# Hybrid conformer/SSD layer on one core: four projection tiles open while h comes in, and x's mean square found token by token

## The chip, the core and the metric

The kernel runs on one core of one Trainium2 chip. The metric is the device time of one execution in microseconds (us); three runs of the kernel before gave 1263.3 to 1267.06 us, with a median of 1263.39 us. The engines are named as in the profile: PE is TensorE, PEld its weight loads, DVE is VectorE, ACT is ScalarE, POOL is GpSimd, and SP is the engine whose queue issues all DMAs here.

## The reference, cut to what matters

One layer of a diffusion backbone with a Conformer branch and a Mamba-2 (SSD) branch, 512 latent tokens x, 256 context tokens ctx, 1024 channels. The change touches the beginning only:

```python
h  = modulate(rmsnorm(x,   norm1_w), mod[0],   mod[1])      # mod   = adaln(c, w_ada, b_ada)
hc = modulate(rmsnorm(ctx, norm1_w), mod_c[0], mod_c[1])    # mod_c = adaln(c_ctx, ...)
proj = h @ w_in                                             # x/B/C, dt, z, GLU and gate columns
xs, B, C, dt_f, dt_b = ssd_inputs(proj)                     # conv of width 5 + SiLU; softplus(dt)
# chunked scan of 8 groups in both directions, starting from the final state of the scan over ctx
```

`rmsnorm(x)` is x / sqrt(mean(x*x over the channels) + 1e-6), times a weight. After the scan come the gated merge, an output projection and a squared-ReLU MLP.

## The kernel before, in words

Channels lie on the partitions and tokens along the free dimension, so a projection tile is 128 output channels by 512 tokens. Each product is made in three passes over exact high and low parts (`gemm`, lines 114 to 116): for each of eight slices k of the input channels, high weights times high activations, high times low, low times high. So a tile of x takes 24 matmuls of 128x512, and a tile of ctx 24 of 128x256. A weight tile comes as `raw` by DMA (line 96, two buffers), ACT casts it to the high part `whi` (line 105), and DVE subtracts to get `wlo` (line 106). `whi` and `wlo` have two buffers each, so a third weight tile can be split only when the products of the first are over.

The order of instructions on each engine is set by a scheduler that works on priorities: normally the order in which the code is written, moved by `later(n)` (what is inside gives way to the next n instructions, and comes earlier for a negative n). Each engine then runs its list strictly as listed.

The beginning: x is loaded (`x_sb`), its squares are added up over the channel tiles into `acc_rx` (line 208), and `rsqrt_mean` turns the sum into 1/sqrt: one matmul with ones sums over the partitions and gives the sum to all 128 of them (`sum`, line 147), and then every step runs on 128x512 elements (`rv` line 133, a square root on ACT, the reciprocal `r` line 136, `rq` lines 138 and 139, `rx` line 142). For ctx the kernel uses `rsqrt_rows` instead: matmuls of 128x1 sum the squares token by token (`rows`, line 157), so that the steps `rt` (lines 161 to 166) run on 128x2 elements, a diagonal matrix `dg` is built (line 168), and a matmul with ones spreads it over the partitions (`spread`, line 171).

The modulation vectors of x and ctx come in four steps, i = 0 to 3. Each step loads a 2 MB block of the adaLN weights (`ablk`, four DMAs, two buffers), makes 32 small matmuls (`aps`, line 252, eight for each DMA, here called a quarter), copies and transposes the result (`arow` on ACT, `apt` on PE), and finishes two channel slices of `mod` on DVE; then `enter` makes the two slices of h (`xr`, `hh` on ACT, `hl` on DVE). Beside the steps three projection tiles are open: dt with step 0, B of group 0 with step 1, C with step 2. Each open tile multiplies the slices of h as they appear. The high and low weights of dt and of B lie in a tile of their own, `wd`, those of C in `whi` and `wlo`. When h is whole, the two x tiles of group 0 (`Xt`, called X0 and X1 below) are made in one go each.

Then every x tile of B, C and X goes through `taps5` on DVE (lines 370 and 374: a convolution of width 5 read from PSUM), hc is made from ctx and `rc`, the ctx tiles follow, and `dt_part` runs a long chain: softplus as a polynomial, running sums `cf` by two scans (lines 327 and 328), their exponential `ecf`, the decays `dec`. `cf` and `ecf` go to DRAM (`s_cf`, lines 343 and 344, four writes for each), the decays too (`s_dec`, lines 346 and 348), and come back spread over the partitions as `decb` (line 349) and, for each head and direction, as `cfb` (line 507, three buffers). In `ssd`, group by group, PE transposes (`bps`, `xps`) and makes states (`sps`) in a PSUM pool of three tiles, ACT copies out (`Bk`, `xt`, `hst`), DVE makes the states that enter the chunks (`hst`, lines 497 and 498, with `decb`), ACT makes the exponents `e` from `cfb` (line 510), POOL and DVE make `Cd` from `cfb` (line 523), and PE makes the outputs `yps` (line 536 from `Cd` and `hst`, line 532 from `e` and `xt`).

The lines that the change touches lie in `rsqrt_rows`, `stat`, the loop of the four steps, and `xbc_first`.

Of the kernel before, what the change touches and what calls it, by code (L numbers as in the profile page):

```python
# [8 lines left out]
F32 = mybir.dt.float32  # L9
# [5 lines left out]
P = 128  # L15
D = 1024
KT = 8
T = 512
TC = 256
# [3 lines left out]
EPS = 1e-6  # L23
# [3 lines left out]
# columns of the packed per-channel vectors  # L27
# [8 lines left out]
# order of the input projection's 128-column tiles  # L36
# [6 lines left out]
# the groups beside which the first tiles of the convolution module run  # L43
GLU_AT = (0, 1, 2, 3, 4)
# the steps of the first modulation vectors beside which the first three weight tiles come, and ctx
BEGIN_AT, CTX_AT = (0, 1, 2), 3
# products that keep the tensor engine's clock up before there is work
WARM = 22
# the products of C and the decays (direction, head of the pair) that VectorE does, the rest are GpSimd's
DECAYS_V = ((0, 1),)  # L50
# how far instructions move in the order of priority
# [5 lines left out]
def build(tc, xT, ctxT, cond, crow, wada1, wada2, vecs, hv, cst, w_in, w_co, w_so, w_o, w_1, w_2, outT):  # L57
    nc = tc.nc
    with ExitStack() as es:
# [26 lines left out]
        @contextmanager  # L86
        def later(n):
            """what is traced inside gives way to the next n instructions"""
            tc.cur_priority += n
            yield  # L90
            tc.cur_priority -= n

# [37 lines left out]
        def rsqrt_mean(ps, n, cnt, r=None):  # L130
            """1/sqrt(sum/cnt + EPS) of a sum broadcast over the partitions"""
# [18 lines left out]
        def rsqrt_rows(parts, n, cnt, pool, out=None):  # L150
            """the same of the sum of several tiles, found token by token and then spread over the partitions"""
            nch = n // P
            s = pool.tile([P, T], F32, name="rows", tag="pm")
            for i, part in enumerate(parts):
                with later(ROWS_LATER):
# [36 lines left out]
        with tc.tile_pool(name="st", bufs=1) as st:  # L192
# [10 lines left out]
            def stat(src, n, acc, out):  # L203
# [5 lines left out]
                if n == TC:  # L209
                    return rsqrt_rows([acc], n, D, pm, out)  # L210
                return rsqrt_mean(allsum(acc, n, pm), n, D, out)
# [12 lines left out]
            # products of nothing: the tensor engine's clock halves when it idles  # L224
# [10 lines left out]

            for i in range(4):
# [3 lines left out]
                if i == BEGIN_AT[0]:  # L240
                    begin(W_DT, py.tile([P, T], F32, name="ps", tag="py"), wd[:, 0], wd[:, 1])
                if i == BEGIN_AT[1]:
                    begin(W_GRP, ps_big(), wd[:, 2], wd[:, 3])
                if i == BEGIN_AT[2]:
                    begin(W_GRP + 1, ps_big())
                if i == CTX_AT:
                    for j, c in enumerate(ctx):
                        nc.sync.dma_start(c, ctxT[:, 2 * j:2 * j + 2])
# [26 lines left out]
        wx = [load_w(w_in[W_GRP + 2 + j], early=0) for j in range(2)]  # L275
# [18 lines left out]
        def dt_part(ps, pc):  # L294
            conv = bigt("conv")
            # rows: heads forward, the same again, heads backward, the same again; the first of each hold
            # chunks 0 to 2, the second chunk 3 and the context
# [10 lines left out]
            # softplus: max(v, 0) + log1p(u), u = exp(-|v|), log1p(u) = 2 atanh(u / (2 + u))  # L308
# [13 lines left out]
            # running sums within the chunks and within the context, backward ones from the end  # L322
# [22 lines left out]
            # step s: chunk s forward, chunk 3 - s backward  # L345
# [41 lines left out]
        def xbc_first():  # L387
            """the first group's, all of x's part before ctx's"""
            Bt, Ct, X0, X1 = (xbc_tile(tag, n) for tag, n in (
                ("Bt", T + TC), ("Ct", T), ("Xt", T + TC), ("Xt", T + TC)))  # L390
            (w_dt, ps_dt, _), (w_b, ps_b, _), (_, ps_c, _) = begun
# [3 lines left out]
            for j, o in enumerate((X0, X1)):  # L395
                ps = ps_big()
                gemm(ps, wx[j], rh)
# [39 lines left out]
        def ssd(g, Bt, Ct, X, Z):  # L437
            ch = lambda t, c: t[:, c * P:(c + 1) * P]
            # B^T C of every chunk, for both directions
# [9 lines left out]
            # B by token  # L449
# [6 lines left out]
            # x by token, and times what reaches the chunk's end  # L456
# [420 lines left out]
```

## Time and profile before

| what | us |
|---|---|
| median of 3 runs (lowest, highest) | 1263.39 (1263.3, 1267.06) |
| span of the profiled execution | 1264.2 |
| PE busy in it | 1220.7 |
| DVE busy | 953.7 |
| ACT busy | 667.4 |
| first product of an open tile starts | 23.43 |
| first product of the SSD outputs (`yps`) starts | 113.69 |

The profiled execution has no time of its own in the list of runs; its span, from the first to the last instruction, stands in its place. PE busy is the union of spans with modelled ends, so that a matmul of 128x512 shows about 0.4 us though the next starts 0.23 us after it. An idle time in a timeline stands in square brackets behind the instruction that ended it, with what released that instruction.

### The profile page before, as it was taken

To read this page: it belongs to the slowest core of one execution; us is meant where nothing else is said; L and a number is where in the kernel's file an instruction comes from. 1 tells how busy PE (TensorE), PEld (TensorE's weight loads), DVE (VectorE), ACT (ScalarE), POOL (GpSimd) and SP (SyncE) were. 2 spreads that over 40 slices of the span, in tenths; PEclk is the share of its full clock that TensorE was granted. 3 is DMA by queue.
4 is the path that set the end of the run, shared out by engine and by line. 5 is a ranking of instruction groups with operands and counts; after the bars stand their busy time and mean duration, and the time that the engine had idled before them with its cause. 6 is when DMAs were issued, how large, how long until landed. Compare 5 with 4: busy or idle time off the path is not lost.

```text
span 1264.2 us, 17493 instructions
## 1 busy us (share of the span) xinstructions
PE 1220.7 (97%) x6665; PEld 995.6 (79%) x6665; DVE 953.7 (75%) x1567; ACT 667.4 (53%) x1124; POOL 108.9 (9%) x74
## 2 busy tenths in 40 slices
PE   6998999999999899999999999999999999999997
PEld 3786778777787778787888877778998888888886
DVE  6797689999999999998999798885843343443444
ACT  4557888686776748868453452134431331331442
POOL 0001222121020302124000000000000000000000
PEclk8999999999999999999999999999999999999999
DMA  9424363343342424333363357964222333233332
GB/s 363 142 67 133 137 198 128 120 146 106 121 159 93 158 83 147 112 134 117 109 193 126 119 188 258 305 196 153 62 65 86 100 100 92 92 100 101 96 104 67
DMA packets 56260, 169.96 MB, mean 134 GB/s; under 512 B 6640, under 2 KB 9584, under 8 KB 56048
## 3 DMA queue, kind: packets, MB, share of 16 engines
q1 hardware_dynamic: 56176, 168.85, 41.0%
q8 instruction: 52, 0.85, 0.3%
q14 instruction: 32, 0.26, 0.1%
HBM read 162.27 MB, written 6.55 MB: 134 GB/s over the span
## 4 chain that ended last, share of the span: by engine, by line
PE 65%; DVE 20%; DMA 8%; issue 3%; ACT 3%; SPq 0%; POOL 0%; DVEq 0%; ACTq 0%; POOLq 0%
PE ps L114 20%; PE ps L115 19%; PE ps L116 19%; DVE conv L575 5%; DVE wlo L106 3%; DVE Xt L374 3%; DMA aw<-in_wada_dram 2%; DMA cfb<-s_cf 2%; PE yps L536 2%; PE yps L532 2%; PE sps L485 1%; DMA yr<-s_y 1%; DVE aw L675 1%; DMA raw<-in_w_dram 1%; ACT whi L105 1%
## 5 line engine op out<-in xcount | busy, mean ns | idle before, releaser
L105 ACT CAST whi<-raw 128x1024 fp32r<-128x1024 f32 x163 | 170.9, 1049 | 320.6 <-PE ps L115 291.5
L106 DVE TENSOR_TENSOR wlo<-raw,whi 128x1024 fp32r<-128x1024 f32 x163 | 203.8, 1251 | 84.3 <-ACT whi L105 76.1
L114 PE MATMUL ps<-hh,whi 128*128 128x512 f32 x632 | 258.0, 408 | 2.3 <-DVE Xt L374 2.1
L116 PE MATMUL ps<-hh,wlo 128*128 128x512 f32 x632 | 255.4, 404 | 2.3 <-DVE wlo L106 2.2
L115 PE MATMUL ps<-hl,whi 128*128 128x512 f32 x632 | 256.7, 406 | 0.0
L575 DVE SCALAR_TENSOR_TENSOR conv<-sg,V,conv 128x480 f32<-128x480 f32 (+14 forms) x240 | 173.3, 740 | 2.6 <-ACT conv L569 1.1
L114 PEld LDWEIGHTS ps<-hh,whi 128*128 128x128 f32 x632 | 119.4, 189 | 30.8 <-issue 7.2
L116 PEld LDWEIGHTS ps<-hh,wlo 128*128 128x128 f32 x632 | 119.4, 189 | 30.7 <-DVE wlo L106 4.7
L115 PEld LDWEIGHTS ps<-hl,whi 128*128 128x128 f32 x632 | 119.6, 189 | 26.5 <-issue 3.7
L711 DVE SCALAR_TENSOR_TENSOR x<-ps,mod,x 128x512 f32<-128x512 f32 (+1 forms) x48 | 31.7, 660 | 100.1 <-PE ps L116 100.1
L510 ACT ACTIVATE e<-cfb,cfT 128x128 f32<-128x128 f32 x256 | 83.9, 391 | 36.8 <-PE yps L532 17.5
L523 POOL TENSOR_TENSOR Cd<-Ct,cfb 128x512 f32<-128x512 f32 x48 | 72.6, 1518 | 313.0 <-DMA cfb<-s_cf 250.3
L116 PE MATMUL ps<-h2h,wlo 128*128 128x512 f32 (+1 forms) x240 | 89.8, 375 | 0.0
L115 PE MATMUL ps<-h2l,whi 128*128 128x512 f32 (+1 forms) x240 | 89.8, 375 | 0.0
L114 PE MATMUL ps<-h2h,whi 128*128 128x512 f32 (+1 forms) x240 | 89.4, 375 | 0.0
L115 PE MATMUL ps<-gl,whi 128*128 128x512 f32 x224 | 88.4, 395 | 0.0
L114 PE MATMUL ps<-gh,whi 128*128 128x512 f32 x224 | 88.2, 394 | 0.0
L116 PE MATMUL ps<-gh,wlo 128*128 128x512 f32 x224 | 87.9, 392 | 0.0
L374 DVE SCALAR_TENSOR_TENSOR Xt<-ps,V,Xt 128x255 f32<-128x255 f32 (+3 forms) x128 | 74.2, 605 | 3.9 <-ACT Xt L370 3.6
L114 PE MATMUL ps<-hc,whi 128*128 128x256 f32 x184 | 52.5, 285 | 3.1 <-DVE Xt L374 3.1
L115 PE MATMUL ps<-hc,whi 128*128 128x256 f32 x184 | 52.4, 285 | 0.0
L116 PE MATMUL ps<-hc,wlo 128*128 128x256 f32 x184 | 52.1, 283 | 0.0
(259 smaller groups left out, 2417.5 us busy)
## 6 DMA issues: line engine op xcount, KB each, us to landing
raw<-in_w_in_dram SPq DMA_DIRECT2D x81, 512.0 KB, 3.6
cfb<-s_cf SPq DMA_DIRECT2D x64, 512.0 KB, 4.4
raw<-in_w_dram SPq DMA_DIRECT2D x64, 512.0 KB, 3.5
aw<-in_wada_dram SPq DMA_DIRECT2D x64, 256.0 KB, 4.3
ablk<-in_wada_dram SPq DMA_DIRECT2D x16, 512.0 KB, 8.6
raw<-in_w_so_dram SPq DMA_DIRECT2D x16, 512.0 KB, 3.7
s_y<-yt SPq DMA_DIRECT2D x16, 256.0 KB, 2.2
yr<-s_y SPq DMA_DIRECT2D x16, 256.0 KB, 3.6
```

What stands on the lines that cost most here:

```text
L105: nc.scalar.copy(hi, raw)
L106: nc.vector.tensor_tensor(lo, raw, hi, ALU.subtract)
L114: nc.tensor.matmul(ps, lhsT=whi[:, k, :], rhs=rhi[:, k, t0:t1], start=start and k == 0, stop=False)
L115: nc.tensor.matmul(ps, lhsT=whi[:, k, :], rhs=rlo[:, k, t0:t1], start=False, stop=False)
L116: nc.tensor.matmul(ps, lhsT=wlo[:, k, :], rhs=rhi[:, k, t0:t1], start=False, stop=stop and k == KT - 1)
L374: nc.vector.scalar_tensor_tensor(o[:, lo:hi], ps[:, lo + d:hi + d], vcol(V_SCW + 5 * ch + j), o[:, lo:hi], ALU.mult, ALU.add)
L510: nc.scalar.activation(ch(e, c), cb_[:, 0, c * P:(c + 1) * P], AF.Relu, bias=cfT[:, c, hd:hd + 1], scale=-1.0)
L523: (nc.vector if (d, r) in DECAYS_V else nc.gpsimd).tensor_tensor(Cd, Ct, cb_[:, 1, :], ALU.mult)
L532: nc.tensor.matmul(o, lhsT=xt[:, c, hr, :], rhs=ch(Ms[r], c), start=False, stop=True, skip_group_check=True)
L536: nc.tensor.matmul(o, lhsT=hst[:, s, k, hr * 64:hr * 64 + 64], rhs=ch(Cs[k][r], c), start=k == 0 and c == 0, stop=False, skip_group_check= ...
L575: nc.vector.scalar_tensor_tensor(o[:, :, lo:hi], u[:, :, lo + d:hi + d], wv(j), o[:, :, lo:hi], ALU.mult, ALU.add)
L711: nc.vector.scalar_tensor_tensor(x1[:, j, a:b], ps[:, a:b], mod[:, gcol + j, 0:1], x1[:, j, a:b], ALU.mult, ALU.add)
```

## The change

It has four parts. `stat` uses `rsqrt_rows` for x too, with a delay of 0 in the order of priority instead of 60. The weights of dt are asked for ahead of the first adaLN block, those of B with step 0, those of C with step 1. A fourth tile, X0 of group 0, is open from step 2 on, in the third and last tile of the PSUM pool `pp` (B and C have the other two, dt is in another pool), so that X1 gets the tile that B's taps have left. X0 is then not made in `xbc_first` any more, and only X1's weights are loaded behind the loop. (In the changed file some lines have moved by one or two, so line 252 is 251 there, 349 is 348.)

```diff
-BEGIN_AT, CTX_AT = (0, 1, 2), 3
+BEGIN_AT, CTX_AT = (-1, 0, 1, 2), 3
...
-        def rsqrt_rows(parts, n, cnt, pool, out=None):
+        def rsqrt_rows(parts, n, cnt, pool, out=None, late=ROWS_LATER):
...
-                with later(ROWS_LATER):
+                with later(late):
...
-                if n == TC:
-                    return rsqrt_rows([acc], n, D, pm, out)
-                return rsqrt_mean(allsum(acc, n, pm), n, D, out)
+                return rsqrt_rows([acc], n, D, pm, out, ROWS_LATER if n == TC else 0)
...
+            begin(W_DT, py.tile([P, T], F32, name="ps", tag="py"), wd[:, 0], wd[:, 1])
             for i in range(4):
...
-                if i == BEGIN_AT[0]:
-                    begin(W_DT, py.tile([P, T], F32, name="ps", tag="py"), wd[:, 0], wd[:, 1])
                 if i == BEGIN_AT[1]:
                     begin(W_GRP, ps_big(), wd[:, 2], wd[:, 3])
                 if i == BEGIN_AT[2]:
                     begin(W_GRP + 1, ps_big())
+                if i == BEGIN_AT[3]:
+                    begin(W_GRP + 2, ps_big())
...
-        wx = [load_w(w_in[W_GRP + 2 + j], early=0) for j in range(2)]
+        wx = [begun[3][0], load_w(w_in[W_GRP + 3], early=0)]
...
-            (w_dt, ps_dt, _), (w_b, ps_b, _), (_, ps_c, _) = begun
+            (w_dt, ps_dt, _), (w_b, ps_b, _), (_, ps_c, _), (_, ps_x, _) = begun
...
             for j, o in enumerate((X0, X1)):
-                ps = ps_big()
-                gemm(ps, wx[j], rh)
+                ps = ps_big() if j else ps_x
+                if j:
+                    gemm(ps, wx[j], rh)
                 taps5(o[:, :T], ps, j, EVICT_FIRST)
```

The priorities of everything behind are the same numbers, but the scheduler lays out the lists anew. Three places follow.

**First place: PE up to the first product of an open tile** (`aps` is a block of adaLN products, `apt` its transpose, `ps<-hh,wd` the first product). Before:

```order
L147 MATMUL sum<-acc_rx,C 128x512
L252 MATMUL aps<-ablk,sc 32x128 x32
L258 MATMUL apt<-C,arow 128x128
L252 MATMUL aps<-ablk,sc 32x128 x24
L114 MATMUL ps<-hh,wd 128x512
```

Now:

```order
L157 MATMUL rows<-C,acc_rx 128x1 x4
L171 MATMUL spread<-dg,C 128x512
L251 MATMUL aps<-ablk,sc 32x128 x32
L257 MATMUL apt<-C,arow 128x128
L251 MATMUL aps<-ablk,sc 32x128 x16
L114 MATMUL ps<-hh,wd 128x512 x2
L115 MATMUL ps<-hl,wd 128x512
```

The one sum of x has become four products of one column and a spread; both stand ahead of the first adaLN block; two quarters of the second block instead of three stand ahead of the first product of dt.

**Second place: PE around the norm of ctx** (`rows<-C,acc_rc` sums the squares of ctx, `spread<-dg,C` spreads the result, `whi` and `wlo` are the weights of C, X0 and X1). Before, the sums, and 26 products of 128x512 counted from the second sum on before the spread:

```order
L114 MATMUL ps<-hh,whi 128x512
L115 MATMUL ps<-hl,whi 128x512
L116 MATMUL ps<-hh,wlo 128x512
L157 MATMUL rows<-C,acc_rc 128x1
L114 MATMUL ps<-hh,whi 128x512
L157 MATMUL rows<-C,acc_rc 128x1
L115 MATMUL ps<-hl,whi 128x512
L116 MATMUL ps<-hh,wlo 128x512
```

Now:

```order
L114 MATMUL ps<-hh,whi 128x512
L115 MATMUL ps<-hl,whi 128x512
L116 MATMUL ps<-hh,wlo 128x512
L157 MATMUL rows<-C,acc_rc 128x1 x2
L114 MATMUL ps<-hh,whi 128x512
L115 MATMUL ps<-hl,whi 128x512
L116 MATMUL ps<-hh,wlo 128x512
L114 MATMUL ps<-hh,whi 128x512
L171 MATMUL spread<-dg,C 128x256
L115 MATMUL ps<-hl,whi 128x512
```

The spread stood behind 26 products after the sums, and now stands behind four, which are the first of X1; on DVE the split of X1's weights stands ahead of the steps from the sums to `dg`, and five taps of B, C and X0 stand between these steps, as five did before.

**Third place: SP's queue and ACT where group 0 begins** (`s_cf`, `s_dec` are the writes of the sums and decays, `decb` and `cfb` the loads of what they wrote, `e` the exponents made from `cfb`). SP before:

```order
L346 DMA s_dec<-dec 32x3
L348 DMA s_dec<-dec 32x1 x3
L343 DMA s_cf<-conv 32x384
L344 DMA s_cf<-conv 32x128
L343 DMA s_cf<-conv 32x384
L344 DMA s_cf<-conv 32x128
L349 DMA decb<-s_dec 128x192
L96 DMA raw<-in_w_in_dram 128x1024
L507 DMA cfb<-s_cf 128x1024 x4
```

SP now:

```order
L342 DMA s_cf<-conv 32x384
L343 DMA s_cf<-conv 32x128
L342 DMA s_cf<-conv 32x384
L343 DMA s_cf<-conv 32x128
L345 DMA s_dec<-dec 32x3
L347 DMA s_dec<-dec 32x1
L507 DMA cfb<-s_cf 128x1024 x2
L347 DMA s_dec<-dec 32x1 x2
L507 DMA cfb<-s_cf 128x1024 x2
L348 DMA decb<-s_dec 128x192
L96 DMA raw<-in_w_in_dram 128x1024
```

ACT before:

```order
L455 COPY Bk<-bps 128x512
L455 COPY Bk<-bps 128x256
L384 ACT_TABLE_LOAD
L384 ACTIVATE Bt<-Bt 128x768
L477 COPY xt<-xps 128x512
L491 COPY hst<-sps 128x512
L477 COPY xt<-xps 128x512
L510 ACTIVATE e<-cfb,cfT 128x128 x5
```

ACT now:

```order
L455 COPY Bk<-bps 128x512
L455 COPY Bk<-bps 128x256
L510 ACTIVATE e<-cfb,cfT 128x128 x4
L512 ACTIVATE e<-e 128x512
L510 ACTIVATE e<-cfb,cfT 128x128 x4
L383 ACT_TABLE_LOAD
L383 ACTIVATE Bt<-Bt 128x768
L477 COPY xt<-xps 128x512 x2
L491 COPY hst<-sps 128x512
```

On SP all eight writes of `s_cf` now stand ahead of the decays, and four loads of `cfb` ahead of `decb`. On ACT eight exponents from `cfb` have moved ahead of SiLU of the next group's B, the copies of `xt` and that of the first state `hst`.

## Rows read from the trace of the kernel before

**Rows 1.** The page, part 1: busy time of each engine, share of the span, instructions.
```profile
PE 1220.7 (97%) x6665; PEld 995.6 (79%) x6665; DVE 953.7 (75%) x1567; ACT 667.4 (53%) x1124; POOL 108.9 (9%) x74
```

**Rows 2.** Windows over the program: stretch, length, busy time (instructions) by engine, TensorE clock, DMA share, GB/s.
```profile
50.00:100.00 50.00, 46.11 (x260) 39.77 (x259) 47.48 (x103) 30.10 (x47) 0.00 (x0) 1.00 0.22 66
...
100.00:150.00 50.00, 45.20 (x271) 34.87 (x270) 37.82 (x66) 38.00 (x81) 9.46 (x7) 0.97 0.47 144
...
150.00:640.00 490.00, 477.93 (x2797) 385.81 (x2796) 458.65 (x736) 357.84 (x665) 92.74 (x60) 1.00 0.40 130
```

**Rows 3.** Timeline of PE, 10 to 24 us: start, length, instruction, idle before and releaser.
```profile
12.04 1.86 PE L147 MATMUL sum<-acc_rx,C 128*128 128x512 f32 x2 [3.82 <-DVE acc_rx L208]
...
13.83 2.85 PE L252 MATMUL aps<-ablk,sc 128*32 128x128 f32 x64
...
17.07 0.33 PE L258 MATMUL apt<-C,arow 128*128 128x128 f32 x1 [0.40 <-ACT arow L256]
...
20.82 0.65 PE L252 MATMUL aps<-ablk,sc 128*32 128x128 f32 x16 [0.64 <-DMA ablk<-in_wada_dram]
...
23.43 0.80 PE L114 MATMUL ps<-hh,wd 128*128 128x512 f32 x1 [1.96 <-ACT hh L217]
```

**Rows 4.** Timeline of DVE (VectorE), 13 to 24 us.
```profile
15.33 3.35 DVE L136 RECIPROCAL r<-r 128x512 f32<-128x512 f32 x1 [0.70 <-ACT r L135]
...
18.60 1.16 DVE L106 TENSOR_TENSOR wd<-raw,wd 128x1024 fp32r<-128x1024 f32 x1
...
21.11 0.69 DVE L142 SCALAR_TENSOR_TENSOR rx<-rq,r 128x512 f32<-128x512 f32 x1
```

**Rows 5.** Windows in the beginning, columns as in rows 2.
```profile
12.00:16.00 4.00, 3.96 (x50) 2.34 (x54) 1.36 (x2) 1.93 (x3) 0.00 (x0) 0.57 1.02 417
...
18.00:22.00 4.00, 1.94 (x48) 1.16 (x48) 3.97 (x8) 0.01 (x1) 0.00 (x0) 1.00 1.04 412
...
24.00:28.00 4.00, 3.56 (x23) 2.52 (x23) 3.67 (x7) 1.30 (x3) 0.00 (x0) 0.50 1.03 410
```

**Rows 6.** Timeline of PE near the end, the last norm.
```profile
1257.43 0.67 PE L171 MATMUL spread<-dg,C 128*128 128x256 f32 x2 [1.88 <-DVE dg L168]
```

**Rows 7.** Timeline of PE, 52 to 60 us, the norm of ctx.
```profile
52.72 0.28 PE L157 MATMUL rows<-C,acc_rc 128*128 128x1 f32 x2
...
58.88 0.60 PE L171 MATMUL spread<-dg,C 128*128 128x256 f32 x2
```

**Rows 8.** Timeline of DVE, 50 to 60 us.
```profile
50.84 0.75 DVE L374 SCALAR_TENSOR_TENSOR Bt<-ps,V,Bt 128x510 f32<-128x510 f32 x1
...
53.64 0.15 DVE L161 TENSOR_SCALAR rt<-rows 128x2 f32<-128x2 f32 x1
...
57.32 0.42 DVE L168 TENSOR_TENSOR dg<-C,rt 128x256 f32<-128x256 f32 x1
```

**Rows 9.** Timeline of SP's queue, 98 to 114 us.
```profile
97.62 1.36 SPq L348 DMA_DIRECT2D s_dec<-dec  x3
...
104.58 0.34 SPq L349 DMA_DIRECT2D decb<-s_dec  x1
...
105.50 2.77 SPq L507 DMA_DIRECT2D cfb<-s_cf  x3
```

**Rows 10.** Timeline of ACT (ScalarE), 98 to 114 us.
```profile
104.30 1.28 ACT L384 ACT_TABLE_LOAD   x1 [0.85 <-DVE Bt L374]
...
107.91 0.58 ACT L491 COPY hst<-sps 128x512 f32<-128x512 f32 x1 [0.89 <-PE sps L485]
...
112.29 1.71 ACT L510 ACTIVATE e<-cfb,cfT 128x128 f32<-128x128 f32 x5 [3.31 <-DMA cfb<-s_cf]
```

**Rows 11.** Timeline of PE, 98 to 114 us, and PE's waits up to 150 us (total, times, longest).
```profile
113.69 0.43 PE L536 MATMUL yps<-Cd,hst 128*64 128x128 f32 x2 [3.15 <-POOL Cd L523]
...
PE yps L536 <- POOL Cd L523: 4.8, 2, 3.1
```

**Rows 12.** DMA issues by line, 90 to 115 us: count, size, median time to landing.
```profile
s_cf<-conv SPq DMA_DIRECT2D x4, 48.0 KB, 3.7
```

## The prediction

> **What bounds the kernel now.** I read the page's busy times first: PE is busy in 97% of the span [rows 1]. Then I read the windows, since an average says nothing of one stage. From 150 to 640 us PE is busy for 477.93 of 490 us [rows 2]: there PE is the bound, and this change alters none of its work there. From 50 to 100 us both PE (46.11 of 50) and DVE (47.48 of 50) are nearly full, and from 100 to 150 us PE stands still for 4.8 us [rows 2]. So a gain at the start is kept only if it reaches about 150 us: past that point PE has its fixed list to work through, and what is saved by then stays saved.
>
> Third, I read the timelines of the beginning. The sum of x's squares is made on PE at 12.04 [rows 3], and 1/sqrt is ready at 21.80, where `rx` ends [rows 4]. In between lie a reciprocal over 128x512 that takes 3.35 us and, in DVE's list, a weight subtraction of 1.16 us that two small steps of the norm stand behind [rows 4]. The first product of an open tile starts at 23.43 [rows 3]. It runs at 1.2 GHz: from 24 to 28 us the granted clock is 0.50, after a stretch in which PE had only quarters of adaLN products with idle times between them (1.94 us busy in 18 to 22) [rows 5].
>
> Last, I read the other end of the beginning. The first load of `cfb` is issued at 105.50, behind `decb` at 104.58, which waited for the decays issued from 97.62 on [rows 9]. It lands when ACT starts on it, at 112.29 [rows 10], and PE, which has waited 3.15 us, starts the outputs of group 0 at 113.69 [rows 11].
>
> **The change, part by part.** The sum is made against the profiled execution, whose span is 1264.2 us; that is 0.8 above the median of the three runs, 1263.39.
>
> *The norm of x.* Four sums of one column replace the sum of 1.86 us. A pair of records takes 0.28 us for one such sum at full clock [rows 7], so four take 0.6 to 1.2; PE has idled for 3.82 us before [rows 3], so I take 1.2: 13.24. Between such sums and a spread PE waited 1.88 us where nothing else was in the way [rows 6]; `dg` for 512 tokens instead of 256 adds about 0.3 (0.42 for 256 columns [rows 8], 0.69 for an operation of 512 [rows 4]). So the spread starts at 15.4 and, priced like the old sum, ends at 17.3. `rx` is there by 18, almost 4 us earlier. But that is not the gain. The first adaLN block now stands behind the spread, so it runs from 17.3 to 20.1 instead of from 13.83 (2.85 us, [rows 3]; 3.5 if PE stays slow). Copy and transpose of it ended 0.7 us behind it, at 17.40 [rows 3]: now 20.8. The path from `rx` to the first product took 1.63 us (21.80 to 23.43), one step of which is no longer in it; I take 1.3. First product at 22.1: **-1.3 us** (bounds -0.6 and -1.9).
>
> *The clock.* PE is now busy almost without a break from 15.4 to 22. I expect it to be at 2.4 GHz when the products start. That saves half of the 4 us at 0.50 [rows 5]: **-2.0** (bounds 0 and -3).
>
> *The loads.* From 12 to 28 us the queues move 410 to 417 GB/s [rows 5], so 512 KB take 1.3 us, and each later adaLN block comes that much later. This costs nothing: PE waited only 0.64 us for the last such quarter before the products [rows 3], and comes to it over 3 us later now. Without that cover it would be 1.3. The Trainium skill ("Perfetto Trace Analysis", the note on HBM above 100%) puts the ceiling of one core's 16 DMA engines at about 435 GB/s; the rows agree, and by it alone fetching ahead would only push other loads back, which would make this part +1.3 instead of 0.
>
> *Four open tiles.* The products are the same 120. By the two lists B is now finished after 84 of them instead of 67 (I counted them to the last product on `wd`). Between the sums of ctx and the spread 26 products took 6.0 us [rows 7], 0.23 each, so 17 more are 3.9 us. One more quarter lies behind the first product (0.65, [rows 3]), and the last block is cut into small pieces, for which I take 0.5 (0 to 1.4). B's taps began at 50.84 [rows 8]; they begin 3.9 + 0.65 + 0.5 - 1.3 - 2.0 = 1.8 us later, at 52.6.
>
> *A new wait.* X0's 24 products used to cover three things: B's taps leaving their PSUM tile for X1, the split of X1's weights, and the steps from the sums of ctx to `dg`, 4.1 us on DVE from 53.64 to 57.74 [rows 8]. Now only four products of X1 stand between sums and spread, so PE will wait at X1's first product and at the spread, 4 us together (bounds 0 and 4.4). Who waits behind it: the rest of X1, then `rc`, hc and every ctx product. X1's products end later, but the spread itself comes only some 0.6 us later, since DVE sets it now as it nearly did before. DVE has 2.5 us of idle in 50 to 100 us [rows 2], and everything it needs lies ready earlier than before (C and X0 end with B); I let it win back the 1.8. So dt's sums end when they did, **0** (bounds -1 and +3.7).
>
> *The queue.* `cfb` needs `s_cf` alone. The eight writes are now in front: four more issues (1.7 us) and a landing of 3.7 [rows 12] from about the time of 97.62 give 103.0, and they no longer queue behind the exponentials of the decays, some 0.5 earlier: 102.5, **-3.0** for the first `cfb` (bounds 0 and -4). It lands at 109.3 instead of 112.29.
>
> *ACT's list.* That is given back. Eight exponents (1.71 us for five [rows 10], so 2.7), one operation of 128x512 (0.6) now come ahead of what ended with the copy of `hst`. That stretch ran from 104.30 to 108.49 with 0.89 of waiting [rows 10], 3.3 net, and a second copy (0.6) joins it. The first state is copied at 109.3 + 2.7 + 0.6 + 3.3 + 0.6 = 116.5, and the next one needs two operations of 0.7 on DVE: 117.9. At that place in its list (a first bundle of outputs, nine more products done) the old kernel was at 113.69 + 0.43 + 9 x 0.46 at half clock = 118.3. So **-0.4**. PE's second wait for `Cd`, 4.8 - 3.15 = 1.65 us [rows 11], has a load behind it that is asked for earlier now: **-1.0** (0 to -1.65).
>
> Behind that the lists keep their shape group by group, and from the LayerNorm of the conv branch on they are the same: 0, with up to 2 either way, as PE has 12 us of idle from 150 to 640 [rows 2] which new lists deal out anew. The sum is -1.4 from 1264.2, and 0.8 less for the median: **1262.0 us**. I count 0.3% (3.8 us) as what a measurement of this kernel can tell from no change.
>
> **The rivals.** *All of it is kept.* If `cfb` lands at 107 or before and the wait at the spread is covered, PE loses the wait of 3.15, the half clock behind it (9 x 0.23 = 2.1) and the second wait of 1.65 [rows 11], 6.9 at most; I take -5.5: 1257.9. For it speaks the gain of 3 us in the queue; against it ACT's list.
>
> *ACT stands in front of a load (slower).* ACT is where PE's next PSUM tile and first state come from, and it now waits for `cfb` with these copies behind it. Before, it had made them by 108.49, 3.8 us ahead of the landing [rows 10]. If `cfb` lands as late as it did, 112.29, the state comes at 119.5 and outputs start at 120.9, 2.6 later than 118.3; PE meanwhile stands at its third state product and restarts at half clock, 2.1 more. That is +4.7: 1268.1. It decides from a landing of about 109.5 on. The Trainium skill ("TensorE: Matmul & The Clock Gate", Architectural detail) says that ScalarE's and VectorE's queues are strictly first in, first out; the subtraction in rows 4 agrees, and by that rule alone this rival would be the outcome whenever the load is late.
>
> *The fourth tile does nothing.* It may only trade X0's cover for an earlier X0 [rows 7, 8], and the start may be lost to DVE's full list: +-0, 1263.4.
>
> **How the numbers follow.** My forecast has 0.47, the gain kept 0.26, ACT's wait 0.19, nothing 0.08. A tail of the forecast on each side passes 0.3%: faster 0.29, same 0.49, slower 0.22. The range takes in the two outer cases: 1256.5 to 1268.
>
> **What would show it.** Right: the first product near 22.1 with a granted clock of 1.00 from 24 to 28; PE waiting some 4 us for DVE at X1 and at the spread; `cfb` issued near 102.5; `hst` copied near 116.5. Wrong: a clock of 0.50 again, no wait at the spread, `cfb` still behind 105, or a difference that arises past 150 us, where I see none.

## The result and the profile after

The changed kernel takes 1270.65 us (median of 20 runs, 1268.06 to 1277.68); the kernel before, run beside it, 1263.74 us (20 runs, 1260.08 to 1273.31). The ratio is 1.005, with a 95% interval of 1.0036 to 1.0063: the change costs 6 us, half a per cent, where 1262.0 with a range of 1256.5 to 1268 was forecast. The profiled execution has a span of 1270.3 us (1264.2 before).

The page, part 1, of the changed kernel [rows 1]: every engine does almost what it did.

```profile
PE 1225.7 (96%) x6673; PEld 999.9 (79%) x6673; DVE 953.9 (75%) x1568; ACT 659.8 (52%) x1119; POOL 110.2 (9%) x74
```

The start, as the timeline of PE shows it [rows 3]:

```profile
12.35 1.87 PE L157 MATMUL rows<-C,acc_rx 128*128 128x1 f32 x8 [4.57 <-DVE acc_rx L208]
...
16.29 2.08 PE L171 MATMUL spread<-dg,C 128*128 128x512 f32 x2 [2.08 <-DVE dg L168]
...
23.88 0.73 PE L114 MATMUL ps<-hh,wd 128*128 128x512 f32 x2 [0.29 <-ACT hh L215]
```

The windows of the start and of 50 to 100 us [rows 5, 2]:

```profile
12.00:16.00 4.00, 1.87 (x8) 1.78 (x8) 1.58 (x7) 2.79 (x5) 0.00 (x0) 0.50 1.03 420
...
24.00:28.00 4.00, 3.42 (x40) 1.97 (x40) 3.46 (x6) 0.53 (x1) 0.00 (x0) 1.00 0.97 348
50.00:100.00 50.00, 43.60 (x222) 36.76 (x221) 43.94 (x94) 29.54 (x46) 0.00 (x0) 0.93 0.13 42
```

The clock is at 2.4 GHz when the products start, as forecast, but the first of them starts at 23.88 instead of 23.43. And from 50 to 100 us, where DVE was nearly full, it now has 6.06 us of idle time instead of 2.52. So I looked for what DVE waits for. Timeline of DVE before, from the last block's `mod` to the last scan of the running sums:

```profile
44.23 0.17 DVE L260 TENSOR_TENSOR mod<-apt,V 128x8 f32<-128x8 f32 x1 [3.98 <-PE apt L258]
...
94.43 0.95 DVE L328 TENSOR_TENSOR_SCAN conv<-conv,dysq 64x384 f32<-64x384 f32 x1
```

and after:

```profile
49.96 0.17 DVE L259 TENSOR_TENSOR mod<-apt,V 128x8 f32<-128x8 f32 x1 [7.83 <-PE apt L257]
...
57.56 1.53 DVE L373 SCALAR_TENSOR_TENSOR Bt<-ps,V,Bt 128x510 f32<-128x510 f32 x2 [1.85 <-ACT Bt L369]
...
102.22 0.95 DVE L327 TENSOR_TENSOR_SCAN conv<-conv,dysq 64x384 f32<-64x384 f32 x1
```

The last `mod` is 5.7 us later, and DVE stands idle for its transpose for 7.83 us; B's taps begin 6.7 us later (50.84 before, [rows 8]); the sums end at 103.17 instead of 95.38, 7.8 us later. One window from the last `mod` to the end of the sums, first before, then after:

```profile
44.23:95.38 51.15, 48.82 (x265) 41.69 (x264) 48.15 (x100) 31.29 (x49) 0.00 (x0) 1.00 0.21 63
```

```profile
49.96:103.17 53.21, 46.81 (x236) 39.40 (x235) 47.05 (x98) 30.11 (x46) 0.00 (x0) 0.94 0.16 49
```

DVE has 47 to 48 us of work there in 51 to 53 us, so most of what is late at the last `mod` is late at the sums. (Over all runs below the stretch takes 50.3 to 55.1 us.) But DVE's wait just ahead of the taps, 1.85 us, is for B itself. B's last product on PE, before and then after:

```profile
49.53 0.39 PE L116 MATMUL ps<-hh,wd 128*128 128x512 f32 x1
```

```profile
55.68 0.39 PE L116 MATMUL ps<-hh,wd 128*128 128x512 f32 x1
```

From the transpose to there PE does not wait in either kernel. So the late `mod` and the late end of B both come from what PE has ahead of them in its list.

The lateness stays. The first product of the SSD outputs starts at 124.55 instead of 113.69, and the sum of the LayerNorm of the conv branch, where PE's list has long been the same in both kernels again, starts 7.0 us later, before and then after:

```profile
715.73 1.02 PE L147 MATMUL sum<-cacc,C 128*128 128x512 f32 x2
```

```profile
722.71 1.02 PE L147 MATMUL sum<-cacc,C 128*128 128x512 f32 x2
```

At the end 6.1 us are left. So the lateness is there at the sums, and nothing is added to it behind 715 us.

Why is the last transpose late? Timeline of PE ahead of it, first before (whole quarters), then after:

```profile
40.61 0.64 PE L252 MATMUL aps<-ablk,sc 128*32 128x128 f32 x16
...
42.55 0.64 PE L252 MATMUL aps<-ablk,sc 128*32 128x128 f32 x16
...
43.69 0.39 PE L114 MATMUL ps<-hh,whi 128*128 128x512 f32 x1
43.92 0.27 PE L258 MATMUL apt<-C,arow 128*128 128x128 f32 x1
43.95 0.47 PE L115 MATMUL ps<-hl,whi 128*128 128x512 f32 x1
44.26 0.39 PE L116 MATMUL ps<-hh,wlo 128*128 128x512 f32 x1
```

```profile
47.21 0.41 PE L251 MATMUL aps<-ablk,sc 128*32 128x128 f32 x2
47.54 0.49 PE L116 MATMUL ps<-hh,wlo 128*128 128x512 f32 x1
47.97 0.41 PE L251 MATMUL aps<-ablk,sc 128*32 128x128 f32 x2
48.30 0.50 PE L114 MATMUL ps<-hh,whi 128*128 128x512 f32 x1
48.73 0.41 PE L251 MATMUL aps<-ablk,sc 128*32 128x128 f32 x2
...
49.64 0.27 PE L257 MATMUL apt<-C,arow 128*128 128x128 f32 x1
```

Before, a quarter of eight adaLN products and five products of 512 columns take 1.94 us (40.61 to 42.55); less five at the 0.23 of such a product, the quarter is just under 0.8 (0.77 in e5's text below). After, one adaLN product and one of 512 columns take 0.76 (47.21 to 47.97), so that the lone one is 0.53. A cut, one more piece of the block among the products, thus costs about 0.5 us. In the profile it shows as busy PE: from 40 to 50 us PE is busy for 10.00 of 10 us in both kernels. There are 18 pieces ahead of the last transpose instead of 11, and 58 products instead of 43: 7 x 0.5 + 15 x 0.23 = 7 us, less about 2 for the clock (an estimate, half of the 4 us at 0.50 in [rows 5]), plus 0.45 for the first product, which makes 5.4; 5.7 are seen. The Trainium skill ("TensorEngine Tiling (Array Packing)", Key Properties) says that a change of the tiling mode, not just of the tile, drains TensorE. The rows fit that: `aps` runs on 128*32 of the array and the products on 128*128, while the full-width transpose at 43.92 costs only 0.1 us (43.69 to 44.26 is 0.57, two products are 0.47). That it is the drain, and not for instance a load of weights that nothing covers, no run here shows.

At group 0, on SP, ACT and PE [rows 9 to 11]:

```profile
107.69 0.82 SPq L507 DMA_DIRECT2D cfb<-s_cf  x2
...
119.51 0.32 SPq L348 DMA_DIRECT2D decb<-s_dec  x1
```

```profile
114.29 1.28 ACT L510 ACTIVATE e<-cfb,cfT 128x128 f32<-128x128 f32 x4 [3.61 <-DMA cfb<-s_cf]
...
120.40 0.60 ACT L491 COPY hst<-sps 128x512 f32<-128x512 f32 x1
```

```profile
62.56 0.74 PE L114 MATMUL ps<-hh,whi 128*128 128x512 f32 x1 [3.43 <-DVE rt L165]
...
120.08 4.54 PE L485 MATMUL sps<-xw,Bk 128*128 128x256 f32 x12 [3.35 <-ACT xt L477]
124.55 0.44 PE L536 MATMUL yps<-Cd,hst 128*64 128x128 f32 x4
```

`cfb` is issued 4.5 us behind the sums instead of 10.1: the queue's gain is 5.6 us, but it is counted from sums that are 7.8 us late. PE waits 3.43 us at X1, as forecast, and 3.35 us for ACT's copies. `decb`, now behind four loads of `cfb`, is issued at 119.51 instead of 104.58. Counted from the end of the sums the outputs start 3.1 us later than before, 21.4 instead of 18.3.

### The profile page after: what moved, and what is told of

It is laid out like the page before. It is cut to its first block, busy times and chain, and to the rows that moved or that the text cites. A ratio compares the mean times of both kernels' runs of the same rounds, so it can differ in the third digit from the quotient of the medians.

```text
span 1270.3 us, 17519 instructions
## 1 busy us (share of the span) xinstructions
PE 1225.7 (96%) x6673; PEld 999.9 (79%) x6673; DVE 953.9 (75%) x1568; ACT 659.8 (52%) x1119; POOL 110.2 (9%) x74
## 4 chain that ended last, share of the span: by engine, by line
PE 61%; DVE 21%; DMA 9%; issue 4%; ACT 4%; POOL 1%; SPq 0%; DVEq 0%; ACTq 0%; POOLq 0%
PE ps L115 18%; PE ps L116 18%; PE ps L114 18%; DVE conv L575 6%; DVE wlo L106 4%; DMA aw<-in_wada_dram 2%; DMA cfb<-s_cf 2%; DVE Xt L373 2%; PE sps L485 1%; DVE e L513 1%; PE yps L536 1%; DMA yr<-s_y 1%; PE yps L532 1%; ACT whi L105 1%; DVE e L520 1%
## 5 line engine op out<-in xcount | busy, mean ns | idle before, releaser
L575 DVE SCALAR_TENSOR_TENSOR conv<-sg,V,conv 128x488 f32<-128x488 f32 (+14 forms) x240 | 180.6, 769 | 1.5
L373 DVE SCALAR_TENSOR_TENSOR Xt<-ps,V,Xt 128x510 f32<-128x510 f32 (+3 forms) x128 | 74.4, 606 | 1.9 <-ACT Xt L369 1.8
L115 PE MATMUL ps<-hc,whi 128*128 128x256 f32 x184 | 53.1, 288 | 0.0
L115 PEld LDWEIGHTS ps<-h2l,whi 128*128 128x128 f32 x240 | 45.1, 188 | 9.0 <-DVE h2l L757 0.8
```

Of the source, the lines that this page charges most:

```text
L115: nc.tensor.matmul(ps, lhsT=whi[:, k, :], rhs=rlo[:, k, t0:t1], start=False, stop=False)
L373: nc.vector.scalar_tensor_tensor(o[:, lo:hi], ps[:, lo + d:hi + d], vcol(V_SCW + 5 * ch + j), o[:, lo:hi], ALU.mult, ALU.add)
L575: nc.vector.scalar_tensor_tensor(o[:, :, lo:hi], u[:, :, lo + d:hi + d], wv(j), o[:, :, lo:hi], ALU.mult, ALU.add)
```

## The experiments

I began with four theories. A: the last adaLN block is late, behind more products and its own cuts, and DVE with it. B: PE's wait at X1 and at the norm of ctx. C: the lists of group 0, with exponents and `cfb` ahead of what PE waits for. D: the new norm of x. All ratios are to the kernel before on the same chip, with 95% intervals. "Ahead" counts products and pieces of adaLN blocks ahead of the last transpose; the two times are read from each run's timeline of DVE as above.

| kernel | ahead | last `mod` | sums end | ratio |
|---|---|---|---|---|
| before | 43, 11 | 44.23 | 95.38 | 1 |
| changed | 58, 18 | 49.96 | 103.17 | 1.0050 (1.0036 to 1.0063) |
| e1, e14: norm alone | 43, 12 | 42.99, 43.83 | 94.11, 94.92 | 0.9968 (0.9953 to 0.9983), 0.9989 (0.9972 to 1.0006) |
| e2: tiles alone | 57, 17 | 50.33 | 103.17 | 1.0051 (1.0032 to 1.0069) |
| e3: not ahead | 43, 13 | 44.93 | 100.07 | 1.0003 (0.9986 to 1.0019) |
| e4: products later | 55, 12 | 45.38 | 95.63 | 0.9987 (0.9970 to 1.0004) |
| e5: e2, whole | 56, 11 | 46.55 | 99.19 | 1.0054 (1.0035 to 1.0073) |
| e6: e1, cut | 45, 21 | 47.99 | 98.72 | 1.0031 (1.0015 to 1.0046) |
| e7: three tiles | 47, 11 | 43.59 | 94.20 | 0.9958 (0.9942 to 0.9973) |
| e8, e11: changed, whole | 57, 12 | 47.02, 46.84 | 99.66, 99.48 | 1.0024 (1.0007 to 1.0041), 1.0023 (1.0007 to 1.0039) |
| e9: changed, own tile | 58, 18 | 48.82 | 101.78 | 1.0054 (1.0033 to 1.0076) |
| e10: both | 57, 12 | 46.62 | 99.86 | 1.0034 (1.0013 to 1.0054) |
| e12: both, other lists | 57, 12 | 47.26 | 98.71 | 1.0024 (1.0009 to 1.0039) |
| e13: e1, late transpose | 54, 12 | 46.49 | 99.21 | 1.0012 (0.9996 to 1.0029) |
| e15: e7, C later | 43, 12 | 44.56 | 95.71 | 1.0003 (0.9983 to 1.0023) |

**Parts alone.** e1 is the kernel before with the new norm only:

```diff
-                return rsqrt_mean(allsum(acc, n, pm), n, D, out)
+                return rsqrt_rows([acc], n, D, pm, out, 0)
```

> Only the norm of x is found token by token; three open tiles and their weights as before. In PE's list the last adaLN transpose stands behind 43 products, as before, and group 0's lists on SP and ACT read as before. Theory A (the last adaLN block comes late, so B's taps and DVE's full list begin late): last transpose at 43 to 45 us, B's taps at 50 to 52, time within 2 us of the kernel before. Theory B (the wait of PE at X1 and at the norm of ctx): no such wait here, same time. Theory C (group 0's lists, exponents ahead of copies and four cfb ahead of decb): same time. Theory D (the new norm of x itself costs, since the first adaLN block stands behind the spread): first product at 23.9 and 1266 or more.

Measured: 1258.8 us. D falls: the norm is a gain, though of uncertain size; the same kernel on another chip (e14, below) gave 1262.15.

e2 is the opposite, the changed kernel with the old norm of x.

> Four open tiles with their weights ahead, but the old norm of x. The last adaLN transpose stands behind 57 products and its block in pieces (17 instead of 11); group 0's lists on SP and ACT read as before the change (no exponent ahead of the copies, no cfb ahead of decb); the spread of ctx stands behind 9 products. Theory A: last transpose at 48 to 50 us, B's taps at 56 to 58, dt's sums end at 101 to 104 and the time is 1268 to 1271. Theory B: PE waits 3 us or more at X1, time 1266 to 1268. Theory C: time as before, 1263 to 1265. Theory D: time as before.

Measured: 1269.43 us. The tiles with their early weights lose as much without the new norm, and with the lists of group 0 as they were before: C isn't needed. The norm's gain, on the other hand, doesn't show in the changed kernel: its sums end when e2's do, at 103.17, and its ratio is the same.

e3 is the changed kernel with every weight load one step later:

```diff
-BEGIN_AT, CTX_AT = (-1, 0, 1, 2), 3
+BEGIN_AT, CTX_AT = (0, 1, 2, 3), 3
```

> Four open tiles and the new norm, but each tile's weights one step later (dt with step 0, X0 with step 3). The last transpose stands behind 43 products again, the spread of ctx behind 20; group 0's lists keep eight exponents ahead of the copies and four cfb ahead of decb. Theory A: last transpose at 44 to 46 us, B's taps at 51 to 53, time 1262 to 1265. Theory B: PE's wait at X1 falls under 2 us, time 1265 to 1268. Theory C: the loss stays, 1268 to 1271, with hst copied 7 us or more behind the landing of cfb.

Measured: 1263.38 us. The transpose is back behind 43 products and the loss is gone, though four `cfb` stay ahead of `decb` and eight exponents ahead of the copies: C falls as the cause. But DVE's lateness is not gone: the last `mod` is 0.7 us late and the sums end 4.7 us late, with 1.69 us of waiting for a product of PE and 1.69 for a cast of ACT in between. This is won back behind the sums, in groups whose lists differ from the kernel's before: from the sums to the LayerNorm's sum, `sum<-cacc`, e3 takes 614.5 us and the kernel before 620.3. How much of that is the lists isn't shown, since two traces of one kernel (e8 and e11) differ by some 3 us over the same stretch.

e4 is the changed kernel with `BEGIN_LATER = 150` instead of 60.

> The changed kernel, but the products of the open tiles give way by 150 instead of 60. The last transpose stands behind 55 products instead of 58, its block is in 12 pieces instead of 18, the spread of ctx behind 16 products instead of 4, and group 0's lists read as before the change. Theory A: last transpose at 46 to 48 us, B's taps at 54 to 56, time 1266 to 1269. Theory B: no wait at X1, time 1264 to 1266. Theory C: time 1263 to 1265, with the last transpose as late as it may be.

Measured: 1262.1 us, below the 1266 to 1269 of A and below B's and C's times too. The last `mod` is only 1.2 us late and the sums 0.3. Its last block has 12 pieces instead of 18; that turned me to the cuts.

**The cuts.** e5 is e2 with the last block's quarters kept whole:

```diff
-                    for j in range(4):
-                        nc.tensor.matmul(
+                    with later(-20 if i == 3 else 0):
+                        for j in range(4):
+                            nc.tensor.matmul(
...
```

> As e2 (four tiles, weights ahead, old norm), but the four quarters of the last adaLN block each stay whole: 11 pieces ahead of the last transpose instead of 17, 56 products instead of 57; B still ends with the 84th product, and the lists of SP, DVE and ACT are the same but for a few rows. Price of a piece from the trace of the changed kernel: a lone adaLN product between two products of 512 columns moves PE on by 0.76 us with the product behind it, so 0.53 for itself, while a whole quarter of eight takes 0.77; so a cut costs 0.5. Theory A (the cuts are PE time): 6 cuts, 3.0 us, last transpose near 47 instead of 50.0, time 1266.4, ratio to before 1.003. Rival B (PE's wait for B's taps at the first product of X1, and the norm of ctx behind it): the wait stays, and all of the loss but what the cuts give directly, 3.2 us. Rival E (the loss is that B ends 17 products later, the cuts are hidden because DVE waits for the loads of ctx or for B anyway): unchanged, 1269.4, ratio 1.005.

Measured: 1267.99 us, ratio as e2's. In the profile the last `mod` comes 3.8 us earlier and the sums end 4.0 us earlier, as A says, but the ratio does not show it; the two intervals leave room for at most about 3 us. Taken alone this run speaks against A. Two things on record bear on it, and neither explains it. The profiled execution is the fastest of e5's eight, 1263.94 us, 4 us under their median. And e8 below, on the same chip, differs from e5 in the norm of x alone and has its last `mod` and its sums within 0.5 us of e5's, but its ratio is 0.0030 lower, some 4 us, with a mean granted clock of 0.990 against e5's 0.988. So these times leave some 4 us of a kernel's time unexplained.

e6 is the mirror: e1, and each adaLN product of the last block inside `later(9 if i == 3 else 0)`, so that the block is cut.

> As e1 (three tiles, new norm of x alone), but the last adaLN block cut into pieces: 21 ahead of the last transpose instead of 12, 45 products instead of 43; B still ends with the 67th product, and the lists of SP, DVE and ACT are the same but for a few rows. Theory A: 9 cuts of 0.5 are 4.5 us of PE; last transpose 5 us later than 42.68, B's taps 4.5 later than 49.6, time 1263.3, ratio to before 1.0005. Rival E (cuts are hidden): as e1, 1258.8, ratio 0.997.

Measured: 1264.9 us. Nine cuts, and two products more ahead of the transpose, take the ratio from 0.9968 to 1.0031, some 8 us, and from e14's 0.9989, on another chip, some 5; expected 4.5. This is the clearest run for the cuts: neither interval of e1 or e14 reaches e6's. DVE in e1, then in e6:

```profile
42.99 0.17 DVE L258 TENSOR_TENSOR mod<-apt,V 128x8 f32<-128x8 f32 x1 [3.98 <-PE apt L256]
...
93.16 0.95 DVE L326 TENSOR_TENSOR_SCAN conv<-conv,dysq 64x384 f32<-64x384 f32 x1
```

```profile
47.99 0.17 DVE L259 TENSOR_TENSOR mod<-apt,V 128x8 f32<-128x8 f32 x1 [8.65 <-PE apt L257]
...
97.77 0.95 DVE L327 TENSOR_TENSOR_SCAN conv<-conv,dysq 64x384 f32<-64x384 f32 x1
```

The last `mod` is 5.0 us later: two products more and nine cuts of 0.5. DVE wins back 0.4 of it. It doesn't wait for B here, so the late `mod` alone makes it late.

e8, and again e11, is the changed kernel with e5's edit.

> The changed kernel with the quarters of the last adaLN block whole: 12 pieces instead of 18, 57 products, B ends with the 84th, spread of ctx behind 9 products; the lists of group 0 come out as before the change. Theory A: 3.0 us less than the changed kernel from the cuts, and some 0.5 to 1 less from the spread: 1266.5 to 1267.5 by the time of 1270.65, ratio 1.0025. With the gain of the new norm that e1 showed (4 us) added in full: 1262.4. What stays above e1 is then the wait of 3.4 us at X1 (B). Rival E: as the changed kernel, ratio 1.005.

Measured: 1263.96 us, 3.3 us under the changed kernel by the ratios, near the cuts' 3.0; e11, on another chip, has the same ratio, though each interval just overlaps that of the changed kernel.

e7 is the change without the fourth tile: new norm, weights ahead, three tiles.

> The change without the fourth tile: new norm, weights asked for ahead of the adaLN blocks, three tiles. 47 products and 11 pieces ahead of the last transpose, B ends with the 68th product, the spread of ctx stands behind 17 products; three loads of cfb ahead of decb. Theory A: no cuts and B not late, so as e1: B's taps near 49.6, time 1258.8, ratio 0.997 (within 1.5 us). Rival F (fetching ahead takes the queue from the adaLN blocks, 512 KB or 1.3 us each): 1260 to 1262. Rival C (the lists of group 0 with cfb ahead of decb): 1262 or more.

Measured: 1256.64 us, the fastest kernel here, below both kernels of the comparison; it ran on one chip only. F is not seen, and C falls again: group 0's lists have changed here too, PE's 3.15 us of waiting for the first `Cd` [rows 11] is gone, and only 0.34 us for a state of DVE is left there. What e7 has over e1 comes behind the sums: these end at 94.20 and 94.11, and `sum<-cacc` starts at 708.32 and 710.67.

**X1's tile.** e8 is still 7 us above e1 (4 above e14, the same kernel) and 8 above e7, so B was tested. In e9 X1 gets a PSUM tile that is free, and the spread of ctx stands behind X1's products:

```diff
-            nc.tensor.matmul(o, lhsT=ones, rhs=dg.rearrange("p c t -> p (c t)"), start=True, stop=True)
+            with later(100 if n == TC else 0):
+                nc.tensor.matmul(o, lhsT=ones, rhs=dg.rearrange("p c t -> p (c t)"), start=True, stop=True)
...
-                ps = ps_big() if j else ps_x
+                ps = py.tile([P, T], F32, name="ps", tag="py") if j else ps_x
...
-            pc = py.tile([P, T], F32, name="ps", tag="py")[:, :TC]
+            pc = ps_big(TC)
```

> The changed kernel, but X1 gets a PSUM tile that is free (that of the warm-up products at the start), so that it need not wait for B's taps, and the spread of ctx gives way to X1's products: it stands behind 23 products after the sums instead of 4. B's end (84th product) and the cuts of the last adaLN block (18 pieces) stay; the lists of group 0 come out as before the change. Theory B (the wait at X1 is half of the loss): PE's wait of 3.43 us at X1's first product goes, and with it the half clock behind it (3.4 us at 1.2 GHz, worth 1.7): 3.4 to 5.1 us less than the changed kernel, 1265.5 to 1267.2, ratio 1.001 to 1.0025. Theory A alone (cuts and B's late end, DVE's taps late): PE waits for DVE at the next place instead, ratio 1.005 as the changed kernel.

Measured: 1267.18 us, ratio 1.0054. PE in e9:

```profile
59.23 0.50 PE L116 MATMUL ps<-hh,wlo 128*128 128x512 f32 x1 [0.29 <-DVE wlo L106]
...
68.06 0.80 PE L114 MATMUL ps<-hc,wd 128*128 128x256 f32 x2 [3.13 <-ACT hc L216]
```

The wait of 3.43 is gone from X1 and stands at the first ctx product, 3.13 us long. B, which had 1.001 to 1.0025, falls: PE waits for what DVE's list makes, wherever it stands.

e10 is e9 with whole quarters, e11 is e8 again on the same chip, and e12 is e10 without the delay of the spread.

> As e9, and the quarters of the last adaLN block whole: 12 pieces instead of 18, nothing else moved. Theory A and B together: 3.0 us less than e9, and both kernels of the change's two costs gone: ratio 0.997 to 0.9995. B alone: as e9. Rival E (cuts hidden): as e9.

> The same kernel as e8 beside e9 and e10 on one chip: the last block whole, X1 behind B's taps. e8 gave 1.0024 with a third of a per cent of uncertainty. Theory B: 3.4 to 5 us above e10. Theory A alone: as e10, 3 us under e9.

> As e10, but the spread of ctx keeps its place in the order of priorities: it stands behind 21 products instead of 23, and the lists of group 0 change to three loads of cfb ahead of decb and four exponents ahead of the first copy of hst, much like e7's. If those lists are a gain by themselves, as e7 (ratio 0.9958 against e1's 0.9968) suggests: 1 to 3 us under e10, ratio 0.995 to 0.998. If they are a loss (theory C, which e3 and e7 speak against): 3 us above e10.

Measured: 1264.85, 1264.09 and 1263.46 us, which can't be told apart. X1's own tile brings nothing that shows (e10 against e11); e10 is below e9 by some 2.5 us, near the price of the cuts, though the intervals overlap widely; and the lists of group 0 move nothing that shows. The gains that had been expected of e10 (0.997 to 0.9995) and e12 (0.995 to 0.998) did not come.

**The transpose alone.** What keeps e8 above three tiles? A has a second half, 14 more products ahead of the transpose. In e13, e1's kernel, only the last transpose gives way:

```diff
-                nc.tensor.transpose(pt[:, :P], rows, ident)
+                with later(20 if i == 3 else 0):
+                    nc.tensor.transpose(pt[:, :P], rows, ident)
```

> As e1 (three tiles, new norm alone), but the transpose of the last adaLN block gives way: it stands behind 54 products instead of 43, with the quarters whole. PE has the same work and no new piece; only DVE gets the last slices' modulation later, 11 products of 0.23 us or 2.5 us, and B ends with the 71st product instead of the 67th. Theory G (the time at which DVE gets the last modulation sets the end, since DVE works from there to dt's sums almost without idle time): modulation near 45.5 instead of 42.99, sums 2.5 us later, near 96.6, time 2.5 to 3 us above e1, ratio 0.9988. Rival (only PE's own time counts, the cuts and the waits at X1): as e1, 0.9968.

> The same kernel as e1, beside e13 on one chip: ratio 0.9968 within its uncertainty. By theory G 2.5 to 3 us under e13; by the rival level with it.

Measured: 1265.69 against 1262.15 us. PE's products are the same and no block is cut, and the ratio goes from 0.9989 to 1.0012, 2.9 us (2.5 to 3 expected; the intervals overlap, so this rests on the timelines as much). DVE in e14, then in e13:

```profile
43.83 0.17 DVE L258 TENSOR_TENSOR mod<-apt,V 128x8 f32<-128x8 f32 x1 [3.98 <-PE apt L256]
...
93.97 0.95 DVE L326 TENSOR_TENSOR_SCAN conv<-conv,dysq 64x384 f32<-64x384 f32 x1
```

```profile
46.49 0.17 DVE L259 TENSOR_TENSOR mod<-apt,V 128x8 f32<-128x8 f32 x1 [0.57 <-PE apt L257]
...
55.30 0.75 DVE L373 SCALAR_TENSOR_TENSOR Bt<-ps,V,Bt 128x510 f32<-128x510 f32 x1 [2.79 <-ACT Bt L369]
...
98.26 0.95 DVE L327 TENSOR_TENSOR_SCAN conv<-conv,dysq 64x384 f32<-64x384 f32 x1
```

The last `mod` is 2.7 us later and the sums 4.3: DVE also waits 2.79 us for B, which ends with the 71st product instead of the 67th. In the changed kernel B's wait is 1.85. And PE in e13 waits for the slices of h that follow the late `mod`:

```profile
48.20 0.73 PE L114 MATMUL ps<-hh,wd 128*128 128x512 f32 x2 [1.74 <-ACT hh L215]
```

So a late transpose also makes B end late, and this run doesn't tell the two apart.

e15 is e7 with C's weights one step later.

> As e7 (three tiles, new norm, weights ahead), but the weights of C are asked for one step later. The last transpose stands behind 43 products instead of 47 (12 pieces instead of 11), the spread of ctx behind 26 instead of 17, and the lists of group 0 are those of before. Theory G: modulation 0.4 to 1 us earlier than in e7 and sums with it, but the two waits of group 0 come back: ratio 0.9955 to 0.997. If e7's gain over e1 is the fetching ahead alone: 0.9958. If it is the lists of group 0: as e1, 0.9968.

Measured: 1263.9 us, ratio 1.0003, above all that had been expected (0.9955 to 0.997 by G). Its last `mod` came 1.0 us later than e7's, not earlier, and its sums end 0.3 us behind the kernel before's, so the time fits the sums though the forecast of the sums was wrong. Fetching the weights of dt and B ahead shows no gain by itself; what e7 has over the norm alone is not settled.

Over the 17 pairs of times in the table, a straight line of the ratio against the end of the sums has a slope of 1.1 us for each us. The largest misses are 4.0 us (e5), 3.4 (e3) and 2.6 (e7), so a good part of a difference of 6 us can lie elsewhere in a single run. The theory that stands is A, the second half included: what PE has ahead of the last transpose, products and cuts, sets when DVE gets what its long stretch needs, and most of that lateness is still there at the end. The sharper form of it (G in the texts above), that the last modulation sets the end, is shown in e6, where DVE doesn't wait for B. In the changed kernel, e2, e5 and e8 to e13 DVE also waits for B, 1.6 to 2.8 us and behind its wait for `mod`; there the two are not separated.

## Why the prediction was wrong

- *The norm of x*, "first product at 22.1: -1.3 (bounds -0.6 and -1.9)": it was +0.45. PE was at 1.2 GHz from 12 to 16 us (granted clock 0.50), so the sums took 1.87 instead of the 1.2 that I took, and the adaLN block behind the spread 3.55 instead of 2.85; squares that came 0.3 later make up the rest. Part of this is the chance of one execution: in e1 the four sums took 1.05 us and the first product started at 22.61, -0.8 and within the bounds; in e14, the same kernel, 1.87 and 23.44. As a part the norm was a gain, or at least no loss: 0.9968 and 0.9989 with it alone, the second interval reaching past 1.
- *The clock*: right, 1.00 from 24 to 28.
- *The loads*: 0 as forecast; e7 fetches ahead and loses nothing.
- *Four open tiles*: this is the step that failed most. The 17 products more to B's end were right. "Cut into small pieces, for which I take 0.5 (0 to 1.4)" was seven cuts of 0.5 us, 3.5: I had no row for a cut. With 3.5 for 0.5 and +0.45 for -1.3 my own sum gives 3.9 + 0.65 + 3.5 + 0.45 - 2.0 = 6.5; B's taps came 6.7 later.
- *A new wait*, "4 us together (bounds 0 and 4.4)": right in size, 3.43, but all of it at X1 and none at the spread, and without consequence: taken from X1 it came back at the first product of ctx (e9).
- "I let it win back the 1.8. So dt's sums end when they did, 0 (bounds -1 and +3.7)": wrong, and the mechanism with it. I looked at DVE's idle time behind 50 us. But DVE's stretch begins with the last `mod` and with B, it already waited 3.98 us for `mod` before, and from there it has 47 to 48 us of work in 51 to 53. It won back nothing and lost 1.1 more: the sums end +7.8. The term ahead and this one together are the forecast's error: a lateness of 1.8 us that I let vanish was 7.8 us at the sums, and 6.3 us of loss were left in the time.
- *The queue* and *ACT's list*: right in mechanism, wrong in the balance of -0.4. Counted from the sums, `cfb` is issued 5.6 us earlier (3.0 forecast), and `hst` is copied at 120.40, 3.9 behind my 116.5 with sums that are 7.8 late; but the outputs start 3.1 us later, counted so. My sum left out `decb`, which now stands behind four loads of `cfb`, for one of which SP waits 3.5 us for ACT's exponents: DVE waits 4.19 us for `decb` and makes the first of its states at 124.39. At 715 us nothing of this is left: the changed kernel is 7.0 us late there, less than at the sums.
- The rivals: *ACT stands in front of a load* came true as a place (PE waits 3.35 for the copy of `xt`; the landing came at 114.29, past its point of 109.5), but not as the cause of the loss, since e2 loses the same without it. That the cause would be PE's order ahead of the last transpose stood in none of the cases.

## What to carry over

Before costing what overlaps in a stretch, find the instructions with which the bounding engine's nearly unbroken run begins, here the last `mod` and B's first tap, and ask first what the change puts ahead of them, even work that has to be done anyway. Here small products on part of the array were cheap in a run and dear when strewn among full ones, and the busy share did not show it; the starts of consecutive instructions did. A wait that was removed on an engine that only follows came back at the next place (e9).

## What was not expected of the hardware

A lone adaLN product on 128*32 of the array between two on 128*128 moved PE on by 0.53 us, where eight in a run take just under 0.8. And the late kernel also ran at a lower clock: the mean granted clock of the changed kernel's 20 runs is 0.988, and 0.991 for 31 runs of the kernel before that were taken with e1 to e4. In the profiled executions the difference lies from 50 to 100 us (1.00 before, 0.93 after), and there behind the new waits of PE:

```profile
60.00:70.00 10.00, 7.44 (x26) 5.83 (x27) 9.85 (x24) 4.38 (x8) 0.00 (x0) 0.83 0.15 52
...
80.00:90.00 10.00, 7.03 (x30) 5.47 (x29) 9.49 (x16) 7.58 (x10) 0.00 (x0) 0.83 0.19 52
```

Both stretches lie ahead of the end of the sums. So what the lower clock costs is part of the 7.8 us there and doesn't come on top of it; how large a part was not tried.
